# Reordering the output projection of the mixing stage inside a hand-ordered attention loop

## The chip, the cores and the metric

One core of one Trainium2 chip runs the whole program. The metric is the device time of one execution in microseconds. The engines are named as in the profile: PE is TensorE (matrix multiplications), DVE is VectorE, ACT is ScalarE, POOL is GpSimd, and SP issues the loads of the weights.

## The reference

Two transformer blocks run one after the other on 512 tokens of width 1024. The change lies in the first block, in its mixing stage. There the normed and modulated tokens `hx` go through `w_mix_in`; 512 of the columns become queries (8 heads of 64), 256 become two heads of keys and values, and 1536 feed a gated short convolution. The attention result `a` (512 wide) and the convolution's result `sc` (512 wide) are normed separately, laid side by side and multiplied by `w_mix_out` (1024 by 1024):

```python
a = latent_attention(apply_rope(q, cos, sin), apply_rope(k, cos, sin), v, kc, vc)
sc = gb * short_conv3(gc * u, conv_w[l])
mix = jnp.concatenate([rmsnorm(a, attn_out_norm[l]), rmsnorm(sc, conv_out_norm[l])], axis=-1)
x = x + m[:, :, 5] * (mix @ w_mix_out[l])
```

So the product falls into two halves that may be added to `x` in either order: the attention's half uses rows 0 to 511 of `w_mix_out`, the convolution's half rows 512 to 1023. What follows is a gated feed-forward layer (`w_ffn2_in`, `w_ffn2_out`) on the normed `x`.

## The kernel before

All of it is one function, `build`, that issues instructions in an order written out by hand; each engine runs its own in that order. `x` is held transposed as `xT` (8 blocks of 128 features by 512 tokens). Tokens 0 to 255 are the slice `XA`, tokens 256 to 511 the slice `XB`. A product in full precision is made of three half-precision ones, so a block of 128 outputs of one half of `w_mix_out` (`mm3`, four pairs of operands) takes 12 matmuls: of 512 columns for all tokens, of 256 columns for one slice.

**Weights.** `wload` puts a unit of 1 MB into a queue. A load starts when one of two staging buffers is free. `pump_one` issues one step of a unit's split into high and low parts: two on ACT (high), two on DVE (low), and after the last one the staging buffer goes to the next load. A split needs one of four (later six) free result buffers, and `done` frees one. `pump_split` issues a whole split. The order of the queue around the change: nine units of `w_mix_in`, the units `("mixo", 1, n)` (convolution's half of `w_mix_out`), then `("mixo", 0, n)` (attention's half), then the feed-forward's `("f2", ch, g)`.

**The attention loop.** It has 35 iterations, i = 0 to 34, for 4 tiles of 128 tokens by 8 heads. Iteration i issues the scores of pair i (PE, then the row maximum on DVE, line 1092), the exponential of pair i-1 (ACT), the transposition of pair i-2 (six on PE into banks 4 and 5, each bank of three copied out as a high part by ACT and a low part by DVE), and the product with the values of pair i-3 (18 matmuls of 64 columns on PE). Between the transpositions and the product with the values it calls `step(gm)` twice, and at its end `pump_one` once, except in the iterations listed in `NOP`. In the iterations listed in `SK` no `step(gm)` is done.

**The generator `gemms`** is what `step(gm)` advances, by one `yield` each. It computes the convolution's branch (48 yields), the sum of squares over features (a product with `ones`, then `Sqrt`, then two reciprocals of 256 tokens on DVE), the scaling and split of the branch's four blocks (`k`), and the convolution's half of `w_mix_out` in eight blocks (`n`): `mm3` in one yield, and in the next the DVE operation `stt(xT[:, n], ...)` that scales the product and adds it to `xT`. Within the loop every product of `gemms` goes to one PSUM bank, number 7 (`gbk.items[:] = [banks[7]]`). Counting the yields: 16 are used ahead of the loop, and two in each iteration outside `SK`. The product with `ones` falls in iteration 19, the `Sqrt` in 20, the reciprocals in 20 and 21, the scalings in 22 to 25, the convolution's half in 26 to 33, with `mm3` in the first step of each iteration and its scaling in the second. `at_T(0)` and `at_T(1)`, the transpositions of the attention's first two tiles, lie in iterations 22 and 23. They use banks 4 and 5 in turn with the loop's transpositions.

**Behind the loop** come `squares` and `norm_at` for tiles 2 and 3, then `proj(n, XA)` for n = 0 to 7 over eight banks, each a block of the attention's half for the first 256 tokens (12 matmuls of 256 columns, the scaling on DVE, and the square on ACT that POOL adds to the sum of squares), with `at_T(2)` and `at_T(3)` between them. Then `pump_lo` finishes an open split, and `proj(n, XB)` runs for n = 0 to 7, with `rstd(XA)` behind n = 0 and the norm of the next stage's `XA` between the others (`modnorm_x`), and one `pump_split` at n = 7. Then `ffn("f2")` begins.

Of the kernel before, what the change touches and what calls it, by code (L numbers as in the profile page):

```python
# [20 lines left out]
T = 512  # L21
# [38 lines left out]
Z = (8, 2, 2, 2, 2)  # L60
PL = (0, 1, 0, 1)
SK = (4, 10, 15)
NOP = (17, 18, 19, 20, 21)
TWO = ()
FX, NP1, NP2 = 3, 2, 1
WP1, WP3 = 2, 1
NDT = 4
# [150 lines left out]
def build(tc, A, cst, coff, uoff, out, stop=None, dbg=None):  # L218
# [8 lines left out]
    V, S, G, PE, SP = nc.vector, nc.scalar, nc.gpsimd, nc.tensor, nc.sync  # L227
# [5 lines left out]
    def al(n, top=False):  # L233
        n = max(8, -(-n // 8) * 8)
        for i in (range(len(holes) - 1, -1, -1) if top else range(len(holes))):
            o, m = holes[i]
            if m >= n:
                if top:
                    holes[i] = (o, m - n)
                    b = Buf(arena[:, o + m - n:o + m], o + m - n, n)  # L240
                else:
                    holes[i] = (o + n, m - n)
                    b = Buf(arena[:, o:o + n], o, n)
                if holes[i][1] == 0:
                    holes.pop(i)
                return b
        raise MemoryError(f"arena: {n} wanted, {holes}")

    def fr(*bs):
        for b in bs:  # L250
            holes.append((b.off, b.n))
        holes.sort()
        i = 0
        while i + 1 < len(holes):
            if holes[i][0] + holes[i][1] == holes[i + 1][0]:
                holes[i] = (holes[i][0], holes[i][1] + holes[i + 1][1])
                holes.pop(i + 1)
            else:
                i += 1
# [5 lines left out]
    banks = [psum[:, i] for i in range(8)]  # L265
# [38 lines left out]
    def stt(o, a, s, b, op0, op1):  # L304
        V.scalar_tensor_tensor(o, a, s, b, op0=op0, op1=op1)  # L305
# [112 lines left out]
    def wload(key, scale=WS):  # L418
        n, src = unit(key)
        info[key] = (n, scale)  # L420
        q_load.append((key, lambda b: SP.dma_start(b.f(n), src)))
# [14 lines left out]
    rst = al(768).f(768)  # L436
# [15 lines left out]
    xT, cT = b_x.f(KT, T), b_c.f(KT, TC)  # L452
# [28 lines left out]
    XA, XB, XC = slice(0, 256), slice(256, 512), slice(512, 768)  # L481

    def ssq(r_, src, first, e=None):
        if first:
            act(r_, src, AF.Square)
        else:
            t = tmp()[:, :src.shape[-1]]
            act(t, src, AF.Square)
            tt(r_, r_, t, ADD, e)
# [38 lines left out]
    def step(g, n=1):  # L528
        for _ in range(n):
            if next(g, 1):  # L530
                return

    def drain(g):
        for _ in g:
            pass
# [198 lines left out]
    b_raw, b_hl, b_got, pp = [], [], [], [0, 0]  # L734
# [100 lines left out]
        wload(("mix", ch))  # L835
    for t in range(2):
        for n in range(2):
            wload(("mixo", 1 - t, n))
    for ch in range(11):
        for g in range(2):  # L840
            wload(("f2", ch, g))
# [54 lines left out]
    GE_ = [G if x else V for x in PL]  # L896
    tbk, rbk, gbk = Rot(banks[0:4]), Rot(banks[4:6]), Rot([banks[2], banks[3], banks[0], banks[1]])
# [84 lines left out]
    for a in range(2):  # L982
        b = tbk()
# [7 lines left out]
    for a in range(NT):  # L991
        b, b2 = tbk(), tbk()
# [19 lines left out]
    b_gc, b_cu, b_sc = al(2 * 512), al(4 * 514), al(2048)  # L1012
    cu, scn = b_cu.f(4, 514), b_sc.f(4, T)
# [4 lines left out]
    def gemms():  # L1018
        for kind, ch in (("c", 5), ("u", 7), ("c", 6), ("u", 8), ("b", 3), ("b", 4)):
            w = need(("mix", ch))  # L1020
            for q in range(2):
                b, w_, x_ = gbk(), wk(w, KT, 256, P * q), hk(hx)
                mm3(b, w_[0:4], x_[0:4], True, False)
                yield
                yield
                mm3(b, w_[4:8], x_[4:8], False, True)
                yield
                n = 2 * ((ch - 3) % 2) + q
                if kind == "c":
                    act(b_gc.f(2, 512)[:, q], b, scale=IW)  # L1030
                elif kind == "u":
                    stt(cu[:, n, 1:513], b, IW, b_gc.f(2, 512)[:, q], MUL, MUL)
                    act(scn[:, n], cu[:, n, 1:513], scale=col("conv_w", 4 + n))
                    stt(scn[:, n], cu[:, n, 0:512], col("conv_w", n), scn[:, n], MUL, ADD)
                    stt(scn[:, n], cu[:, n, 2:514], col("conv_w", 8 + n), scn[:, n], MUL, ADD)
                else:
                    stt(scn[:, n], b, IW, scn[:, n], MUL, MUL)
                    ssq(rst[:, 0:512], scn[:, n], n == 0, GE_[0])
                if q:
                    done(("mix", ch))  # L1040
                yield
        yield
        b, r_ = gbk(), rst[:, 0:512]
        mm(b, ones, r_)
        squares([0, 1])
        yield
        yield
        act(r_, b, AF.Sqrt, bias=eps, scale=1.0 / 512)
        norm_at(0, 2)
        V.reciprocal(rst[:, XA], rst[:, XA])  # L1050
        yield
        yield
        V.reciprocal(rst[:, XB], rst[:, XB])
        yield
        for k in range(4):
            t = tmp()
            stt(t, scn[:, k, :], col("conv_out", k), r_, MUL, MUL)
            split(t, h2[0][:, 4 + k], h2[1][:, 4 + k], GE_[3])
            yield
            if k < 2:  # L1060
                at_T(k)
            yield
        for n in range(KT):
            b, w = gbk(), wk(need(("mixo", 1, n // 4)), 4, 512, P * (n % 4))
            mm3(b, w, hk(h2)[4:8])
            yield
            stt(xT[:, n], b, mcv[:, 2, n:n + 1], xT[:, n], MUL, ADD)
            if n % 4 == 3:
                done(("mixo", 1, n // 4))
            yield  # L1070
# [64 lines left out]
    def at_T(a):  # L1135
        at, b = b_at[a].f(512), pbk()
        for k in range(4):
            tr(b[:, P * k:P * k + P], at[:, P * k:P * k + P])
        split(b.rearrange("p (k t) -> p k t", k=4), h2[0][:, 0:4, P * a:P * a + P], h2[1][:, 0:4, P * a:P * a + P])


    def proj(n, cs, b):
        w = wk(need(("mixo", 0, n // 4)), 4, 512, P * (n % 4))
        o = b[:, 0:256]
        mm3(o, w, hk(h2, cs)[0:4])
        stt(xT[:, n, cs], o, mcv[:, 2, n:n + 1], xT[:, n, cs], MUL, ADD)
        ssq(rst[:, cs], xT[:, n, cs], n == 0, G)

    gm, qh = gemms(), q_heads(0)
    step(gm, Z[0])  # L1150
# [12 lines left out]
    for i in range(8 * NT + 3):  # L1163
        if i < 8 * NT:
            sc_.append(scores(i // 8, i % 8))
        if sc_ and i:
            ex.append(expo(*sc_.pop(0)))
        if ex and i > 1:
            pt_.append(ptrans(*ex.pop(0)))
        fill = i not in SK  # L1170
        step(gm, fill)
        if i < 24 and i % 8 == 0:
            qh = q_heads(1 + i // 8)
        step(gm, fill)
        if pt_ and i > 2:
            pv(*pt_.pop(0))
        step(qh)
        for _ in range(0 if i in NOP else 2 if i in TWO else 1):
            pump_one()
    drain(gm)  # L1180
    squares([2, 3])
    norm_at(2, 2)
    mbk = Rot([banks[i] for i in (7, 0, 1, 2, 3, 6, 7, 0)])
    for n in range(8):
        proj(n, XA, mbk())
        if n == 2:
            at_T(2)
        if n == 5:
            at_T(3)
    checkpoint("sc", b_sc.f(2048))  # L1190
    checkpoint("mx", h2[0])
    fr(b_ro, b_t1, b_t2, *b_q2, b_k2, b_k, b_sm, b_rp, b_gc, b_cu)
# [3 lines left out]
    na, mbk = None, Rot([banks[i] for i in (1, 2, 3, 0, 5, 6, 7, 2)])  # L1196
# [55 lines left out]
    b_lg = al(8 * 12, top=True)  # L1252
# [10 lines left out]
    b_kc, b_cn, b_T, b_gu, b_r2, b_M, b_Q = al(8), al(512), al(768), al(512), al(512), al(512), al(1024)  # L1263
# [172 lines left out]
    for a, _ in enumerate(tokproj("rv", hx, range(NT), to_act(rv))):  # L1436
# [4 lines left out]
        else:  # L1441
            d = a - 2
            b = sb_()
# [54 lines left out]
    b_la, b_lac, b_gk, b_gqT, b_gkc, b_L = (al(n) for n in (2048, 1024, 1024, 1024, 512, 6 * P))  # L1498
# [9 lines left out]
    b = sb_()  # L1508
# [8 lines left out]
    for i in range(2):  # L1517
        b = tb()
        n = 4 - 2 * i
# [5 lines left out]
    for i in range(6):  # L1525
        b = lbk()
# [24 lines left out]
    b_A, b_qd = [al(512) for _ in range(2)], [al(512) for _ in range(2)]  # L1551
# [45 lines left out]
    b_e = [al(512) for _ in range(2)]  # L1597
    for a, _ in enumerate(tokproj("gk", hx, range(NT), to_act(gk))):
        step(rc)
        if a < 2:  # L1600
            o = la[:, 2 * a:2 * a + 2]
            tt(o, o, t6[a + 1], SUB)
        if a == 1:
            fr(*b_t6[1:])
            b_yr = al(2048)
            yr = (b_yr.h(4, T), b_yr.h(4, T, at=4 * T))
    units_done("gk")
    w = need(("in", 8))
    for p in range(2):
        b = pb()  # L1610
# [10 lines left out]
    b_gvc, b_gv, b_gkT = al(1024), al(2048), al(1024)  # L1621
    gvc, gv, gkT = b_gvc.f(2, 512), b_gv.f(NT, 512), b_gkT.f(2, T)
    bSG = {(0, 0): al(512), (1, 3): al(512)}
# [83 lines left out]
    b_gg = al(2048)  # L1707
# [82 lines left out]
    for n in range(KT):  # L1790
        w = wk(need(("wout", n // 2)), KT, 256, P * (n % 2))
        b = pb()
# [4 lines left out]
            pump_one()  # L1797
    drain(gc_)
    checkpoint("yg", yg[0])
    fr(*b_A, *b_km, *b_qm, *b_e, b_yr, b_gv, b_gg, b_la, b_gqT, b_gkT, *b_X, *bSG.values(), b_T, b_gu, b_lg)  # L1800

    ring(spl_free, len(spl_free) + 2)
    coef(0, "norm2", m23, 4, 0)
# [149 lines left out]
    gbk = Rot(banks[4:8])  # L1953
# [432 lines left out]
        tail_T(KT - 1, a)  # L2386
    tail_out([1, 2, 3])
    es.close()
    print('pp', pp)

# [23 lines left out]
```

## Time and profile before

| | |
|---|---|
| median of 3 runs | 2669.93 us (2669.27 to 2672.03) |
| profiled execution | 2673.24 us, span 2671.5 us |
| PE busy | 2597.3 us (97%) |
| DVE busy | 2017.4 us (76%) |
| ACT busy | 1070.0 us (40%) |
| POOL busy | 534.0 us (20%) |
| mean granted PE clock | 0.994 |

The busy shares are means over the span. In the slices of the page PE is at nine tenths nearly everywhere; the attention loop lies at about 648 to 789 us, and what the change touches lies between 715 and 860 us. Times in the rows count from the span's start. A bracket at the end of a timeline's line gives how long the engine idled ahead of it and what released it.

### The profile page before, as it was taken

The numbers are of one execution on the slowest core, as the hardware profiler recorded it, in microseconds if no ns is written. First come the engines' busy times: TensorE is split into PE (matmuls) and PEld (weight loads), VectorE is DVE, ScalarE is ACT, GpSimd is POOL, SyncE is SP. The second block draws the span as 40 slices with busy tenths as digits, with TensorE's granted clock in tenths as the row PEclk, the third lists the DMA queues.
The fourth block names the chain that finished last, engine by engine and source line by source line (L and its number), as shares of the span: only waits on it lengthen the run. The fifth ranks groups of instructions, "written<-read, shape, count | busy, mean of one in ns | idle before, by whom it ended". The sixth has DMA issues, their size and how long they took to land. (4 is left out here: it accounts for less than half of the span.)

```text
span 2671.5 us, 43737 instructions
## 1 busy us (share of the span) xinstructions
PE 2597.3 (97%) x17395; PEld 1650.2 (62%) x17395; DVE 2017.4 (76%) x3604; ACT 1070.0 (40%) x1671; POOL 534.0 (20%) x637
## 2 busy tenths in 40 slices
PE   7999999999989999999999999999999999999998
PEld 3666666675566444479787655576566666666665
DVE  6888547876877786676535787998799777787885
ACT  3544322145655443543434675344333222222224
POOL 1000000001011000011002476123223333333330
PEclk9999999999999999999999999999999999999999
DMA  6698628522105788744211598778999999999982
GB/s 271 225 340 333 216 107 302 188 75 99 49 33 213 278 310 289 271 164 137 74 64 48 194 374 291 275 283 290 375 372 370 395 353 353 349 357 364 357 305 82
DMA packets 209585, 656.09 MB, mean 246 GB/s; under 512 B 19010, under 2 KB 85348, under 8 KB 188900
## 3 DMA queue, kind: packets, MB, share of 16 engines
q1 hardware_dynamic: 156388, 452.68, 46.0%
q0 software_dynamic: 44352, 188.76, 20.1%
q10 hardware_dynamic: 8640, 11.85, 1.2%
q8 instruction: 136, 2.23, 0.3%
q14 instruction: 69, 0.57, 0.1%
HBM read 549.81 MB, written 103.42 MB: 245 GB/s over the span
## 5 line engine op out<-in xcount | busy, mean ns | idle before, releaser
L279 PE MATMUL psum<-arena 128*128 128x384 f16 (+8 forms) x16840 | 2549.3, 313 | 43.1 <-ACT arena L293 21.7
L279 PEld LDWEIGHTS <-arena 128*128 128x128 f16 x16116 | 1500.8, 98 | 925.3 <-issue 24.5
L293 ACT ACTIVATE arena<-arena 128x1024 f16<-128x1024 f32 (+11 forms) x1026 | 743.4, 765 | 1170.0 <-DVE arena L305 922.1
L305 DVE SCALAR_TENSOR_TENSOR arena<-arena 128x1024 f16<-128x1024 f32 (+7 forms) x1240 | 1065.4, 895 | 137.9 <-ACT arena L293 114.6
L308 DVE TENSOR_TENSOR arena<-arena 128x1024 f16<-128x1024 f16 (+11 forms) x668 | 377.6, 589 | 116.1 <-ACT arena L293 98.3
L293 ACT ACTIVATE arena<-psum 128x512 f32<-128x512 f32 (+8 forms) x522 | 263.4, 528 | 403.2 <-PE psum L279 328.4
L308 POOL TENSOR_TENSOR arena<-arena 128x8 f32<-128x8 f32 (+4 forms) x284 | 191.8, 702 | 743.3 <-ACT arena L293 283.3
L305 DVE SCALAR_TENSOR_TENSOR arena<-psum,arena 128x384 f32<-128x384 f32 (+4 forms) x293 | 171.7, 589 | 216.0 <-PE psum L279 178.5
L2166 POOL DMA_INDIRECT arena<-in_peer_down_dram,arena x128 | 130.7, 1021 | 291.2 <-DVE arena L2172 263.4
L2166 POOL DMA_INDIRECT arena<-in_peer_up_dram,arena x128 | 126.6, 989 | 228.8 <-DVE arena L305 216.0
L2172 DVE SCALAR_TENSOR_TENSOR arena<-arena 128x1024 f32<-128x1024 f32 x128 | 155.9, 1219 | 2.1 <-DMA arena<-in_peer_down_dram,arena 2.0
L425 POOL DMA_DIRECT2D arena<-in_units_dram x52 | 27.9, 536 | 645.9 <-DVE arena L305 640.6
L279 PEld LDWEIGHTS psum<-arena 128*128 128x128 f32 (+1 forms) x724 | 94.1, 185 | 48.5 <-issue 19.4
L282 PE MATMUL psum<-arena 128*128 128x128 f32 (+2 forms) x555 | 76.7, 269 | 23.1 <-DVE arena L308 14.6
L282 PEld LDWEIGHTS psum<-arena 128*128 128x128 f32 (+1 forms) x493 | 57.2, 141 | 29.7 <-DVE arena L308 13.3
L1915 DVE MAX8 arena<-arena 128x8 f32<-128x128 f32 (+1 forms) x192 | 42.9, 260 | 36.1 <-POOL arena L308 31.2
L2104 POOL COPY arena<-arena 128x128 f32<-128x128 f32 x24 | 45.9, 1940 | 114.3 <-ACT arena L293 114.3
L308 DVE TENSOR_TENSOR arena<-psum,arena 128x384 f16<-128x384 f32 (+3 forms) x95 | 52.3, 579 | 17.5 <-ACT arena L293 9.2
L1918 DVE FIND_INDEX8 arena<-arena 128x8 uint32<-128x128 f32 (+1 forms) x192 | 47.9, 264 | 0.0
L293 ACT ACT_TABLE_LOAD x33 | 42.3, 1283 | 11.1 <-PE psum L279 8.5
L293 ACT ACTIVATE arena<-psum,arena 128x768 f32<-128x768 f32 (+4 forms) x54 | 39.6, 735 | 12.6 <-PE psum L279 6.6
L1092 DVE TENSOR_REDUCE arena<-psum 128x1 f32<-128x768 f32 x32 | 30.4, 950 | 6.8 <-PE psum L279 6.8
(54 smaller groups left out, 212.8 us busy)
## 6 DMA issues: line engine op xcount, KB each, us to landing
arena<-in_units_dram SPq DMA_DIRECT2D x91, 1024.0 KB
arena<-dscr SPq DMA_DIRECT2D x128, 512.0 KB
arena<-in_units_dram SPq DMA_DIRECT2D x128, 512.0 KB
arena<-in_down_t_dram SPq DMA_DIRECT2D x120, 512.0 KB
dscr<-arena SPq DMA_DIRECT2D x120, 512.0 KB
arena<-in_units_dram POOLq DMA_DIRECT2D x52, 1024.0 KB
gscr<-arena SPq DMA_DIRECT2D x12, 1920.0 KB
arena<-gscr SPq DMA_DIRECT2D x30, 768.0 KB
```

Source lines behind the costliest of these rows:

```text
L279: PE.matmul(o, l, r, start=start, stop=stop)
L282: PE.transpose(o, i, (ident if i.dtype == F32 else ident16)[:i.shape[0], :i.shape[0]])
L293: S.activation(o, i, f, **kw)
L305: V.scalar_tensor_tensor(o, a, s, b, op0=op0, op1=op1)
L308: (e or V).tensor_tensor(o, a, b, op=op)
L425: q_raw.append((key, lambda b: eng.dma_start(b.f(n), src)))
L1092: V.tensor_reduce(n[:, 0:1], s_, axis=mybir.AxisListType.XY, op=ALU.max, negate=True)
L1915: V.max(v[:, c_], x)
L1918: V.max_index(i[:, c_], v[:, c_], x)
L2104: G.tensor_copy(b_Gt[hf].f(NB, 4, 32)[:, nb], Gs[:, 4 * hf:4 * hf + 4])
L2166: G.indirect_dma_start(out=held[job].f(D), out_offset=None, in_=W["peer_up_2" if job[0] else "peer_down_2"], in_offset=bass.IndirectOffset ...
L2172: V.scalar_tensor_tensor(row, row, 1.0, acc, op0=MUL, op1=MUL, accum_out=c_[:, j:j + 1])
```

## The change

The attention's half for `XA` moves from behind the loop into the generator, between the four scalings of the convolution's branch; `proj` writes it into the two halves of bank 7 in turn. The convolution's half comes after it, and its blocks n = 5 to 7 behind the loop, over banks 0, 1, 2, 3, 7. The squares for the sum over `XA` are now taken from the convolution's blocks. The sum of squares of the convolution's branch goes to `b_gc`. The two `mixo` pairs change places in the load queue. `NOP` loses 17 and 18, and from iteration 33 on no step of the generator is made. In a later stage a buffer of 2048 is asked for as two of 1024.

```diff
-NOP = (17, 18, 19, 20, 21)
+NOP = (19, 20, 21)
+END = 33
...
-            wload(("mixo", 1 - t, n))
+            wload(("mixo", t, n))
...
-                    ssq(rst[:, 0:512], scn[:, n], n == 0, GE_[0])
+                    ssq(b_gc.f(512), scn[:, n], n == 0, GE_[0])
...
-        b, r_ = gbk(), rst[:, 0:512]
+        b, r_ = gbk(), b_gc.f(512)
         mm(b, ones, r_)
         squares([0, 1])
         yield
         yield
         act(r_, b, AF.Sqrt, bias=eps, scale=1.0 / 512)
         norm_at(0, 2)
-        V.reciprocal(rst[:, XA], rst[:, XA])
         yield
+        at_T(0)
         yield
-        V.reciprocal(rst[:, XB], rst[:, XB])
+        V.reciprocal(r_[:, XA], r_[:, XA])
+        at_T(1)
         yield
+        V.reciprocal(r_[:, XB], r_[:, XB])
+        yield
+
         for k in range(4):
+            proj(2 * k, XA, half(), False)
+            yield
             t = tmp()
             stt(t, scn[:, k, :], col("conv_out", k), r_, MUL, MUL)
             split(t, h2[0][:, 4 + k], h2[1][:, 4 + k], GE_[3])
             yield
-            if k < 2:
-                at_T(k)
+            proj(2 * k + 1, XA, half(), False)
             yield
         for n in range(KT):
             b, w = gbk(), wk(need(("mixo", 1, n // 4)), 4, 512, P * (n % 4))
             mm3(b, w, hk(h2)[4:8])
             yield
             stt(xT[:, n], b, mcv[:, 2, n:n + 1], xT[:, n], MUL, ADD)
+            ssq(rst[:, XA], xT[:, n, XA], n == 0, G)
             if n % 4 == 3:
                 done(("mixo", 1, n // 4))
             yield
...
-    def proj(n, cs, b):
+    half = Rot([banks[7][:, 0:256], banks[7][:, 256:512]])
+
+    def proj(n, cs, b, last=True):
...
-        ssq(rst[:, cs], xT[:, n, cs], n == 0, G)
+        if last:
+            ssq(rst[:, cs], xT[:, n, cs], n == 0, G)
...
-        fill = i not in SK
+        fill = i not in SK and i < END
...
-    drain(gm)
     squares([2, 3])
     norm_at(2, 2)
-    mbk = Rot([banks[i] for i in (7, 0, 1, 2, 3, 6, 7, 0)])
-    for n in range(8):
-        proj(n, XA, mbk())
-        if n == 2:
-            at_T(2)
-        if n == 5:
-            at_T(3)
+    gbk.items[:] = [banks[i] for i in (0, 1, 2, 3, 7)]
+    step(gm, 6)
+    at_T(2)
+    drain(gm)
+    at_T(3)
...
-            b_yr = al(2048)
-            yr = (b_yr.h(4, T), b_yr.h(4, T, at=4 * T))
+            b_yr = [al(1024) for _ in range(2)]
+            yr = tuple(b.h(4, T) for b in b_yr)
```

## Rows read from the trace of the kernel before

**Rows 1.** The page: span, and busy time of each engine.
```profile
span 2671.5 us, 43737 instructions
PE 2597.3 (97%) x17395; PEld 1650.2 (62%) x17395; DVE 2017.4 (76%) x3604; ACT 1070.0 (40%) x1671; POOL 534.0 (20%) x637
```

**Rows 2.** Windows: stretch, length, PE, PEld, DVE, ACT, POOL busy, PE clock, DMA.
```profile
731.00:744.00 13.00, 7.65 (x74) 5.54 (x74) 10.06 (x14) 9.76 (x17) 1.16 (x1) 0.87 0.00 0
744.00:757.00 13.00, 9.53 (x103) 6.42 (x102) 10.91 (x16) 8.89 (x19) 3.20 (x3) 1.00 0.00 1
757.00:777.00 20.00, 19.90 (x188) 12.38 (x187) 13.51 (x22) 10.93 (x24) 0.76 (x1) 1.00 0.14 53
```

**Rows 3.** Timeline of iterations 21 to 25 (start, length, engine, line).
```profile
737.68 1.74 DVE L1053 RECIPROCAL arena<-arena 128x256 f32<-128x256 f32 x1
...
745.82 0.66 PE L282 MATMUL psum<-arena 128*128 128x128 f32 x4 [1.14 <-DVE arena L308]
...
753.93 1.02 DVE L308 TENSOR_TENSOR arena<-psum,arena 128x384 f16<-128x384 f32 x2
754.87 1.88 DVE L305 SCALAR_TENSOR_TENSOR arena<-arena 128x512 f32<-128x512 f32 x2
756.66 0.95 DVE L1092 TENSOR_REDUCE arena<-psum 128x1 f32<-128x768 f32 x1
```

**Rows 4.** Timeline of iteration 30, with a block of the convolution's half.
```profile
771.70 0.75 DVE L305 SCALAR_TENSOR_TENSOR arena<-psum,arena 128x512 f32<-128x512 f32 x1 [1.36 <-PE psum L279]
...
772.68 0.82 PE L282 MATMUL psum<-arena 128*128 128x128 f32 x6
772.88 0.96 DVE L1092 TENSOR_REDUCE arena<-psum 128x1 f32<-128x768 f32 x1 [0.42 <-PE psum L279]
773.21 0.87 ACT L293 ACTIVATE arena<-psum 128x384 f16<-128x384 f32 x2 [1.08 <-PE psum L282]
...
773.33 3.93 PE L279 MATMUL psum<-arena 128*128 128x512 f16 x34
773.75 1.01 DVE L308 TENSOR_TENSOR arena<-psum,arena 128x384 f16<-128x384 f32 x2
...
776.12 0.75 DVE L305 SCALAR_TENSOR_TENSOR arena<-psum,arena 128x512 f32<-128x512 f32 x1 [1.36 <-PE psum L279]
...
777.30 0.96 DVE L1092 TENSOR_REDUCE arena<-psum 128x1 f32<-128x768 f32 x1 [0.42 <-PE psum L279]
```

**Rows 5.** Timeline behind the loop.
```profile
785.36 7.73 PE L279 MATMUL psum<-arena 128*128 128x512 f16 x84
...
789.20 0.69 DVE L308 TENSOR_TENSOR arena<-psum,arena 128x512 f32<-128x512 f32 x1 [0.19 <-PE psum L279]
...
792.55 1.41 DVE L305 SCALAR_TENSOR_TENSOR arena<-arena 128x512 f32<-128x512 f32 x2
...
793.85 4.09 PE L279 MATMUL psum<-arena 128*128 128x256 f16 x36
...
800.10 0.48 DVE L305 SCALAR_TENSOR_TENSOR arena<-psum,arena 128x256 f32<-128x256 f32 x1
...
803.68 9.87 PE L279 MATMUL psum<-arena 128*128 128x256 f32 x86 [1.37 <-POOL arena L308]
...
806.02 1.75 DVE L495 RECIPROCAL arena<-arena 128x256 f32<-128x256 f32 x1 [0.85 <-ACT arena L293]
```

**Rows 6.** Timeline of the feed-forward's second pair of units.
```profile
838.46 46.78 PE L279 MATMUL psum<-arena 128*128 128x512 f16 x216 [1.04 <-ACT arena L293]
...
840.78 5.77 DVE L305 SCALAR_TENSOR_TENSOR arena<-arena 128x1024 f16<-128x1024 f32 x5 [0.26 <-ACT arena L293]
843.16 0.33 SPq L421 DMA_DIRECT2D arena<-in_units_dram  x1
...
848.99 2.95 ACT L293 ACTIVATE arena<-arena 128x1024 f16<-128x1024 f32 x3 [1.18 <-DMA arena<-in_units_dram]
```

**Rows 7.** Windows of PE alone: stretch, length, busy, PE clock, DMA.
```profile
739.00:744.00 5.00, 3.25 (x28) 0.66 0.00 0
```

More of the change, by code (lines that the diff above doesn't have):

```diff
@@ L1799, in build @@
     checkpoint("yg", yg[0])
-    fr(*b_A, *b_km, *b_qm, *b_e, b_yr, b_gv, b_gg, b_la, b_gqT, b_gkT, *b_X, *bSG.values(), b_T, b_gu, b_lg)
+    fr(*b_A, *b_km, *b_qm, *b_e, *b_yr, b_gv, b_gg, b_la, b_gqT, b_gkT, *b_X, *bSG.values(), b_T, b_gu, b_lg)
     ring(spl_free, len(spl_free) + 2)
@@ L2388, in build @@
     es.close()
-    print('pp', pp)
 _INS = ["q_norm", "k_norm", "attn_out_norm", "ret_decay_f_2", "ret_decay_b_2", "gla_gk_up_f_2", "gla_gk_bias_f_2",
```

## The prediction

> **What bounds the kernel now.** I read the page first: TensorE is busy 97% of the span and no other engine comes near it [rows 1], so a reordering can gain only where TensorE idles or where a chain hangs on one engine. The windows of the attention loop come next [rows 2]: from 731 to 757 us TensorE works 17.2 of 26 us, from 757 to 777 us 19.9 of 20. The first stretch holds the root and the scalings of the convolution's branch, the second the convolution's half of w_mix_out. The reader is to see holes of 8.8 us in the first stretch and none in the second. The timeline gives the reasons. In the holes VectorE sets the pace: from the maximum at 753.02 (one pattern ahead of that at 756.66) an iteration is maximum 0.9, two low parts 0.95, a scaling with a weight's low part 1.8, with no gap, 3.6 us [rows 3]; the reciprocals of 1.74 us and the waits of TensorE for a bank (1.14 us at 745.82) fall there too [rows 3]. In the second stretch an iteration takes 4.42 us from maximum to maximum (772.88 to 777.30), and TensorE has no gap although every block uses one bank: a block's scaling is issued in the same iteration (771.70), long before the next block's multiplication (773.4) [rows 4].
>
> **The change part by part.** Sums are differences inside the profiled execution (2673.24 us, span 2671.5), added to the median of 2669.93, 3.3 us below it.
>
> *Prices.* A block for the first 256 tokens is 12 of the 36 matmuls that took 4.09 us, 1.3 us; a block of the convolution's half twice that, 2.6 us; scalings 0.45 and 0.75 us of VectorE [rows 4, 5]. Eight blocks (10.4 us) go from behind the loop into it; three of the convolution's (7.8 us) go the other way.
>
> *Iterations 20 to 28.* Iteration 20 loses a reciprocal, so the maximum of 21 comes at 734.3 instead of 1.7 us later. Iteration 21 now has both transpositions of tiles 0 and 1 with a reciprocal between their splits. After the maximum VectorE waits to 736.4 for the exponential's table, as it does now, then low parts 1.0, a wait of 0.85 for transposition and copy, split 0.65, reciprocal 1.74 [rows 3], split 0.65: the maximum of 22 at 741.3. From there I add VectorE's own work: 22 has maximum 0.9, low parts 1.0, reciprocal 1.74, projection 0.45, 4.1 in all; 23 and 24 each 0.9, 1.0, 0.7, 0.45 and a weight's low part 1.2, 4.25; 25 has two projections, 2.75; 26 a scaling, a projection and the 0.9 us that closes tile 2, 3.85; 27 3.0. The maximum of 28 comes at 763.5, now at 764.04 (777.30 less three periods [rows 4]). So seven blocks, 9 us of TensorE, disappear in the holes: that is what the change can earn.
>
> *Iterations 28 to 32.* Here the order turns. Counting yields, 62 stand ahead of the convolution's half now and 67 after the change: an odd number. Multiplication and scaling change places: the first step of an iteration scales block n-1, the second multiplies block n, both on bank 7. The multiplication must wait for a scaling that stands on VectorE behind this iteration's maximum and two low parts, which wait for this iteration's transpositions. By iteration 30 [rows 4]: transpositions end at 773.4, low parts at 774.76, the scaling would end at 775.45, the multiplication start at 775.5 in place of 773.4. TensorE idles 2.1 us, and behind it queue the values' product and the next scores, on which the next maximum waits. From multiplication to next maximum it is 3.9 us now, so a period becomes 6.6 to 6.7 instead of 4.42. In 28 the block waits for the last projection's scaling, itself behind the exponential that the last split held up: 767.05 against a free TensorE at 764.35. The maxima: 29 at 771.05 (768.46 now), 30 at 777.75 (772.88), 31 at 784.35 (777.30). From there: wait and block 3 to 5.2, values 0.65, transpositions 0.65, wait 2.1, block 4 2.6, values 0.65, then transpositions, values, a wait of 0.75 for the last low part and the last values: 14.5 us, so the loop ends at 798.9 where it now ends at 789.1 (the closing of tile 3 at 789.20 [rows 5]): **+9.8**.
>
> *The two halves of a bank.* In 25 two projections follow each other in different halves. No row shows a matmul writing one half while VectorE reads the other. If this is free, nothing is added; if the second waits for the first's scaling (755.8 to 756.2 behind the low parts), carrying this through to 29 gives 2.0 us. No row is nearer to either end, so I take the middle, **+1.0**. The Trainium skill, "PSUM — Partial Sum Buffer", section "PSUM bank collisions raise a hardware error", says to guard by bank and quadrant and not by address: by it this term would be 2.0 and the sum 2687. No row shows it.
>
> *Behind the loop.* Now: reciprocal of the first tokens' root at 806.02, 16.9 us after the loop's end [rows 5]. After: block 4's scaling stands behind the norm of tiles 2 and 3, which ends 4.9 us after the loop (the two at 792.55 end at 793.96) [rows 5], so at 5.65. The bank for block 6 is again number 7 (the 20th call takes item 19 modulo 5 of banks 0, 1, 2, 3, 7), so TensorE waits from 2.6 to 5.7. Block 6 to 8.3, block 7 to 10.9, both transpositions to 12.1, split of tile 2 to 12.9, block 7's scaling 13.65, its square 14.1, split of tile 3 15.4, the first block for the last tokens 16.7; the open low part, its scaling, square and root bring the reciprocal to 18.5: **+1.6**. If VectorE holds the split back less, or the wait for bank 7 is covered, it can be 1.5 us below now; the upper end is 3.
>
> *Weights.* Four result buffers stay in use, but the convolution's first unit is freed in iteration 32 instead of 29 and the second behind the loop. So one feed-forward unit fewer is split when that layer starts: two, where there are three now. The second pair starts at 838.46; now its first unit is ready, and the splitting that begins at 840.78 makes its second, whose end at 843.16 starts the next load [rows 6]. After the change that split makes the first: its first half is done at 842.0, so TensorE waits **+3.6**. The load behind it lands in time, as now at 848.99 [rows 6]. Lower end 0, where TensorE's start is already later for its bank; upper end 5. The earlier pump in 18 only moves a split from 25 to 18. The swapped order of the load queue issues the same loads at the same completions, so no queue waits longer. The split buffer of the later stage and the sums on POOL (busy 20% [rows 1]) I cost at nothing; were POOL late, the root behind the loop would wait as it does now (1.37 us at 803.68 [rows 5]).
>
> Sum: 9.8 + 1.0 + 1.6 + 3.6 = 16.0, so **2686 us**. What follows is bound by TensorE for most of its length (97% over the span [rows 1]), so I expect nothing to give it back.
>
> **The rivals.** *Faster:* the wait of the odd order is covered, VectorE reaching the scaling before TensorE needs it, so that blocks 0 to 4 run at 4.42 us an iteration. The loop then ends 0.5 us earlier than now; without the bank wait of block 6 the tail gains 1.5 to 2.6; the low clock of 739 to 744 (0.66 of full over 5 us [rows 7], 1.7 us of work) goes with the fuller holes. That gives 4 to 6 us, 2664. For it speak the holes; against it that low parts and scaling stand on one queue [rows 4]. It decides below a wait of some 0.3 us per block. Chance 0.10. *No change:* the wait is only about 0.5 us, five times 0.5 and 1.6 less the 0.5: some 4 us, 2673.5, the units in time. Chance 0.13. *Clock:* the idle of 2.1 in 6.6 us lowers the clock for the block behind each gap; at half rate a block costs 2.6 more, twice or three times 2.6 us: 2692. Against it: TensorE kept its full clock from 744 to 757 at 9.5 of 13 us busy [rows 2], though it fell just before after idling more [rows 2, 7]. The Trainium skill, "TensorE: Matmul & The Clock Gate", section "A second HAM failure mode: psum-queue depth-cycling", names idling between groups of multiplications as a cause of such swings; by it this case would hold, and the stretch from 744 to 757 does not agree. Chance 0.07.
>
> **How the numbers follow.** The forecast has 0.70. Its own range: the loop 7 to 12, the bank 0 to 2, the tail -1.5 to 3, the weights 0 to 5; not all ends at once, so 2678 to 2691. With part of the no-change case and the clock's, 2673.5 to 2692 holds 8 in 10. A measurement can tell about 0.2%, 5.3 us: faster 0.10, same 0.13, slower 0.77.
>
> **What would show it.** Right: gaps of about 2 us on TensorE, released by VectorE's scaling, in front of blocks 1 to 4; periods near 6.6 us from maximum 29 on; the maximum of 28 hardly moved; a wait of some 3 us for bank 7 behind the loop; a wait of some 3.6 us at the feed-forward's second pair. Wrong: periods of 4.4 us in 29 to 31 with no such gap, or a maximum of 28 more than 3 us off.

## The result and the profile after

The changed kernel takes 2703.99 us (median of 4 runs, 2700.51 to 2704.73) against 2669.88 us before: ratio 1.0122, 95% interval 1.011 to 1.0134. The forecast had the sign and most of the mechanisms, but 16 of 34 us, and the result lies above its range. The span of the profiled execution grows from 2671.5 to 2702.9 us, by 31.4; the account below is made inside the two spans.

The windows of the changed kernel, in the columns of [rows 2], for the same stretches and one more:

```profile
731.00:744.00 13.00, 8.44 (x61) 6.63 (x61) 8.74 (x14) 9.57 (x17) 0.00 (x0) 0.74 0.00 0
744.00:757.00 13.00, 10.55 (x131) 9.14 (x130) 12.61 (x19) 7.99 (x17) 3.21 (x2) 1.00 0.11 33
757.00:777.00 20.00, 16.77 (x171) 12.96 (x169) 11.29 (x21) 7.17 (x16) 2.32 (x2) 0.91 0.08 33
777.00:789.00 12.00, 9.32 (x68) 4.80 (x68) 3.19 (x5) 3.47 (x8) 0.73 (x1) 0.86 0.00 0
```

From 731 to 757 TensorE is now busy 19.0 us where it was busy 17.2. Only part of that is filled holes: from 731 to 744 it runs fewer matmuls than before (61 against 74) and at a lower clock (0.74 against 0.87), from 744 to 757 more of them (131 against 103) at the full clock. But from 757 to 777, where it had no gap, it idles 3.2 us and runs 9% below its full clock; from 777 to 789 VectorE and ScalarE work about 3 us each of 12 and TensorE still idles. So the idle time there is a chain, not a load.

Iteration 25, the timeline of VectorE and TensorE (it has the projections of blocks 3 and 4):

```profile
755.19 1.02 DVE L309 TENSOR_TENSOR arena<-psum,arena 128x384 f16<-128x384 f32 x2
...
756.13 0.48 DVE L306 SCALAR_TENSOR_TENSOR arena<-psum,arena 128x256 f32<-128x256 f32 x1
...
756.66 4.28 PE L280 MATMUL psum<-arena 128*128 128x256 f16 x34 [2.45 <-DVE arena L306]
759.07 0.48 DVE L306 SCALAR_TENSOR_TENSOR arena<-psum,arena 128x256 f32<-128x256 f32 x1 [2.46 <-PE psum L280]
...
760.98 0.96 DVE L1099 TENSOR_REDUCE arena<-psum 128x1 f32<-128x768 f32 x1 [1.43 <-PE psum L280]
761.43 2.65 PE L280 MATMUL psum<-arena 128*128 128x256 f16 x34
```

Block 4's multiplication writes the other half of bank 7, and still starts at 756.66, 0.05 us after the scaling of block 3 ends (756.13 and 0.48). The group then takes 4.28 us; the same 34 matmuls take 2.65 us in the next iteration (761.43). They ran at the lower clock: the granted clock was 0.79 from 754 to 762, in the windows further down.

Iterations 29 and 30, the same view (compare [rows 4]):

```profile
777.65 3.93 PE L280 MATMUL psum<-arena 128*128 128x512 f16 x34 [1.98 <-DVE arena L306]
...
781.62 0.96 DVE L1099 TENSOR_REDUCE arena<-psum 128x1 f32<-128x768 f32 x1 [4.01 <-PE psum L280]
782.00 0.87 ACT L294 ACTIVATE arena<-psum 128x384 f16<-128x384 f32 x2 [3.07 <-PE psum L283]
782.53 1.02 DVE L309 TENSOR_TENSOR arena<-psum,arena 128x384 f16<-128x384 f32 x2
783.47 0.74 DVE L306 SCALAR_TENSOR_TENSOR arena<-psum,arena 128x512 f32<-128x512 f32 x1
784.26 5.61 PE L280 MATMUL psum<-arena 128*128 128x512 f16 x34 [2.03 <-DVE arena L306]
```

Read downward: maximum, high parts, low parts, scaling of the last block, and only then the next multiplication, 2.03 us after TensorE was free. VectorE meanwhile waits 4.0 us for TensorE. Each waits for the other once an iteration. The block behind the third such wait in a row (after those ahead of 771.09 and 777.65) takes 5.61 instead of 3.93 us.

Behind the loop and at the feed-forward's start, the same view:

```profile
804.29 0.69 DVE L309 TENSOR_TENSOR arena<-psum,arena 128x512 f32<-128x512 f32 x1 [0.36 <-PE psum L280]
...
809.77 5.34 PE L280 MATMUL psum<-arena 128*128 128x512 f16 x24 [2.92 <-DVE arena L306]
...
823.21 1.75 DVE L496 RECIPROCAL arena<-arena 128x256 f32<-128x256 f32 x1 [0.85 <-ACT arena L294]
...
837.41 2.92 DVE L306 SCALAR_TENSOR_TENSOR arena<-arena 128x1024 f16<-128x1024 f32 x2 [1.49 <-ACT arena L294]
837.43 0.61 PE L280 MATMUL psum<-arena 128*128 128x256 f16 x2 [4.97 <-ACT arena L294]
...
839.26 22.54 PE L280 MATMUL psum<-arena 128*128 128x256 f16 x189 [1.22 <-DVE arena L306]
...
865.17 0.60 PE L280 MATMUL psum<-arena 128*128 128x512 f16 x2 [3.38 <-ACT arena L294]
866.43 33.93 PE L280 MATMUL psum<-arena 128*128 128x512 f16 x149 [0.65 <-DVE arena L306]
```

Before the change the feed-forward's first product stood at 814.78; the same view of TensorE:

```profile
814.78 5.42 PE L279 MATMUL psum<-arena 128*128 128x256 f16 x48 [1.24 <-DVE arena L305]
```

The last loop output stands 15.1 us later than before (804.29 against 789.20 [rows 5]), the reciprocal 17.2 (823.21 against 806.02 [rows 5]). Then TensorE waits 4.97 and 1.22 us for the two halves of a weight's split (837.41): the feed-forward's first product needs two units, and the second is split only at block 7. After two matmuls at 837.43 it runs from 839.26, where before it ran from 814.78: 24.5 us late. The second pair runs from 866.43, 28.0 us late [rows 6], after waits of 3.38 and 0.65 us for the two halves of its first unit.

The windows of TensorE alone, in the columns of [rows 7], round five places where its clock was low:

```profile
754.00:762.00 8.00, 5.55 (x48) 0.79 0.36 133
784.00:790.00 6.00, 5.74 (x37) 0.72 0.00 0
818.00:824.00 6.00, 5.04 (x31) 0.72 0.40 135
834.00:844.00 10.00, 5.35 (x32) 0.66 0.44 165
865.00:871.00 6.00, 5.18 (x16) 0.72 0.42 113
```

Length times the share missing is about 1.7 us in four of them (8 times 0.21, 6 times 0.28) and 3.4 us in the one from 834 to 844, where TensorE idles nearly half of the time anyway. Each stands behind a wait of TensorE: four behind waits shown above, the one at 818 behind a wait of 2.62 us for ScalarE's split of tile 3.

### The profile page after: what moved, and what is told of

Same layout as the page of the kernel before. It is cut to its first block, busy times and chain, and to the rows that moved or that the text cites. A ratio compares the mean times of both kernels' runs of the same rounds, so it can differ in the third digit from the quotient of the medians.

```text
span 2702.9 us, 43736 instructions
## 1 busy us (share of the span) xinstructions
PE 2607.5 (96%) x17395; PEld 1655.3 (61%) x17395; DVE 2016.3 (75%) x3604; ACT 1069.3 (40%) x1671; POOL 531.3 (20%) x637
## 5 line engine op out<-in xcount | busy, mean ns | idle before, releaser
L280 PE MATMUL psum<-arena 128*128 128x384 f16 (+7 forms) x16840 | 2559.1, 314 | 66.3 <-ACT arena L294 30.2
```

The lines of the kernel that those rows point to most:

```text
L280: PE.matmul(o, l, r, start=start, stop=stop)
```

## The experiments

**One empty step in the kernel before.** Nothing else is changed, so the fuller iterations and the weights' order play no part.

```diff
+        yield
         for n in range(KT):
             b, w = gbk(), wk(need(("mixo", 1, n // 4)), 4, 512, P * (n % 4))
```

> The kernel before with one empty yield ahead of the convolution's half, so that a block's multiplication moves to the second step of an iteration and its scaling to the first step of the next; nothing else. Theory (the odd count is a cost of its own): TensorE waits about 2.0 us for VectorE's scaling ahead of blocks 1 to 7, 14 us, and 0 to 6 us more where the clock falls behind a wait: 2684 to 2691 us. Rival (the waits come from the moved projections or from the fuller iterations, not from the order): within 2 us of 2670.

It took 2687.82 us, ratio 1.007 (1.0053 to 1.0087), and 2690.81 us, 1.007 (1.0047 to 1.0093), in a second set of runs:

> The kernel before with the one empty yield again, beside the run with the filling matmuls on the same chip: 2684 to 2691 us, with two blocks at the low clock.

The timeline of TensorE in the first set:

```profile
775.58 3.92 PE L279 MATMUL psum<-arena 128*128 128x512 f16 x34 [1.98 <-DVE arena L305]
782.14 5.61 PE L279 MATMUL psum<-arena 128*128 128x512 f16 x34 [1.98 <-DVE arena L305]
...
802.24 9.42 PE L279 MATMUL psum<-arena 128*128 128x512 f16 x84 [1.97 <-DVE arena L305]
```

Seven waits of 1.98 us and two groups 1.7 us longer than their likes (5.61 against 3.92, 9.42 against 7.73 [rows 5]). 13.9 and 3.4 make 17.3 of the 18.1 us of the first set. The order of two steps alone does this.

**The same with the waits filled.** Ten matmuls whose results nobody reads, into banks that the next scores overwrite, ahead of each block but the first:

```diff
             b, w = gbk(), wk(need(("mixo", 1, n // 4)), 4, 512, P * (n % 4))
+            for _ in range(10 if n else 0):
+                mm(psum[:, 2 * ((at_i[0] + 1) % 2), 0:384], qT[:, 0, 0:P], kT[:, 0, 0, 0:384])
             mm3(b, w, hk(h2)[4:8])
...
+    at_i = [0]
...
+        at_i[0] = i
```

> The kernel before with the one empty yield, and ahead of blocks 1 to 7 ten more matmuls of 384 columns, 1.6 us, into the banks that the next scores overwrite; their results are not used. They lie inside the wait of 2.0 us. Theory (the clock falls because TensorE idles, and that is 1.7 us each time): all periods from maximum to maximum are 6.6 us, none 8.3, the granted clock stays 1.00 from 760 to 810, 3 us less than the run without these matmuls, 2683 to 2686 us. Rival (the slow block has another cause, or the matmuls only push the waits on): a period of over 8 us remains, 2687 us or more.

2684.22 us (2683.08 to 2685.19), 1.0053 (1.0035 to 1.0071): 3.6 and 6.6 us less than the two sets without them. The times leave it loose, because the intervals overlap and one of the eight executions without the filling took 2683.13 us. The traces, one of each set, say more. The timeline of TensorE:

```profile
775.21 3.92 PE L279 MATMUL psum<-arena 128*128 128x512 f16 x34 [0.36 <-DVE arena L305]
781.77 3.93 PE L279 MATMUL psum<-arena 128*128 128x512 f16 x34 [0.36 <-DVE arena L305]
...
800.19 7.73 PE L279 MATMUL psum<-arena 128*128 128x512 f16 x84 [0.34 <-DVE arena L305]
```

The idle time shrinks to 0.36 us, the starts still stand 6.56 us apart, and both slow groups are gone. The feed-forward's second pair starts at 853.27, in the two sets without the filling at 857.03 and 857.42. One window of TensorE alone, first from this run, then from the second set without the filling:

```profile
783.00:796.00 13.00, 12.30 (x101) 1.00 0.00 0
```

```profile
783.00:796.00 13.00, 9.77 (x76) 0.88 0.01 1
```

So in these traces the low clock is a consequence of the idling, and it is a cost of its own on top of the wait.

**The order restored in the changed kernel.**

```diff
+        yield
         for n in range(KT):
...
-    step(gm, 6)
+    step(gm, 7)
```

> The changed kernel with one empty yield ahead of the convolution's half, which restores multiplication first, scaling second; one block more stands behind the loop. Theory: the waits of 2.0 us ahead of blocks 0 to 4 go, and with them the low clock of block 2 (1.7 us) and the 2.9 us wait for bank 7 behind the loop: 11 to 14 us less, 2690 to 2693 us. Rival (the loss lies in the projections' iterations and the weights): 2701 to 2704 us.

2688.80 us, 1.007 (1.0053 to 1.0086): 15.2 us less than the change, 1.2 more than the expected 11 to 14. All waits ahead of the convolution's blocks are gone, and so is the one for bank 7 behind the loop; the one of iteration 25 and that for the weights stay. The timeline of TensorE:

```profile
756.68 4.28 PE L280 MATMUL psum<-arena 128*128 128x256 f16 x34 [2.45 <-DVE arena L306]
...
775.54 3.93 PE L280 MATMUL psum<-arena 128*128 128x512 f16 x34
...
823.32 0.61 PE L280 MATMUL psum<-arena 128*128 128x256 f16 x2 [4.96 <-ACT arena L294]
825.14 22.80 PE L280 MATMUL psum<-arena 128*128 128x256 f16 x189 [1.22 <-DVE arena L306]
```

**An earlier split in the changed kernel.**

```diff
-PB = (7,)
+PB = (1, 7)
```

> The changed kernel with one more split of a weight unit, at block 1 of the last tokens' projection, where a result buffer is free. Theory (the feed-forward starts 7.3 us late because its second unit is split only at block 7, and its second pair 3.5 us late): both waits go, the split costs about 2.5 us of VectorE in the norm's chain, 7 to 10 us less: 2694 to 2697 us. Rival (the start hangs on the norm's chain, the unit is late without being waited for): 2704 to 2707 us.

2693.08 us, 1.0084 (1.0068 to 1.0101): 10.9 us less, 0.9 more than the expected 7 to 10. The feed-forward starts at 835.81, after a wait of 3.72 us for VectorE (1.24 before), so the split costs 2.5 us in the norm's chain; the second pair starts without a wait for weights. The timeline of TensorE:

```profile
835.81 23.23 PE L280 MATMUL psum<-arena 128*128 128x256 f16 x194 [3.72 <-DVE arena L306]
860.08 20.23 PE L280 MATMUL psum<-arena 128*128 128x512 f16 x93 [1.04 <-ACT arena L294]
```

**Both together,** with `gbk.items` cut to banks 0 to 3 behind the loop.

> The changed kernel with the empty yield ahead of the convolution's half and the earlier split of a weight unit, and bank 7 left out behind the loop. Theory (order and weights are separate costs that add): 15.2 and 10.9 us less than 2704, 2677 to 2680 us, the rest being the two projections of iteration 25 and the split in the norm's chain. Rival (both cure the same lateness at the feed-forward's start): 2686 to 2689 us.

2678.53 us, 1.0033 (1.002 to 1.0046). 15.2 and 10.9 off 2704.0 make 2677.9: within the intervals they add, and are two causes.

**The later stage's buffer,** as two in the kernel before.

> The kernel before with the later stage's buffer of 2048 as two of 1024; nothing else. Theory (it costs nothing): 2669 to 2671 us. Rival (of the 3.4 us that the changed kernel loses after the feed-forward's second pair, a part comes from other addresses): 2672 to 2673.5 us.

2670.74 us, ratio 1.000 (0.999 to 1.001): no cost.

**One projection an iteration.** From the run with both cures: the scaling of a block k ahead of projection k+1, the last three projections with an empty step each, `END = 35`, bank 7 again among the banks behind the loop, and there

```diff
-    step(gm, 7)
-    at_T(2)
-    drain(gm)
-    at_T(3)
+    step(gm, 4)
+    at_T(2)
+    at_T(3)
+    drain(gm)
```

> The same, with at most one projection in an iteration (22 to 29) and the steps of the loop up to its end, so that blocks 0 to 4 of the convolution's half lie in iterations 30 to 34; the transpositions of tiles 2 and 3 go ahead of block 7. Theory (two projections in one iteration cost 2.4 us and a low clock of 1.7 us because both write one bank): 4 to 8 us less than the run without this, 2669 to 2675 us. Rival (the halves of the bank are free of each other, the wait was VectorE's own work): no more than 2 us less.

2672.49 us, 1.001 (1.0001 to 1.0019): 6.0 us less. In the trace the step from maximum 25 to 26 falls from 5.05 us (754.76 to 759.81) to 2.85 us (754.39 to 757.24), so the wait for the bank was worth 2.2 us; the low clock that I had added to it was not there in the run with both cures (its group after the wait took 2.65 us). The other 3.8 us are not traced to one place: this run rearranged the later iterations and the part behind the loop as well, and the second pair starts 4.5 us earlier (844.89 in the run with both cures). So the total does not test the halves; the step does. What is left is a wait of 4.72 us for VectorE ahead of the first product (1.24 before). The second unit's early split now stands in the norm's chain there, 2.36 us of VectorE after 1.13 us of waiting for ScalarE's part; the timeline of VectorE and TensorE:

```profile
810.86 2.36 DVE L306 SCALAR_TENSOR_TENSOR arena<-arena 128x1024 f16<-128x1024 f32 x2 [1.13 <-ACT arena L294]
...
816.11 23.23 PE L280 MATMUL psum<-arena 128*128 128x256 f16 x194 [4.72 <-DVE arena L306]
840.39 39.87 PE L280 MATMUL psum<-arena 128*128 128x512 f16 x184 [1.04 <-ACT arena L294]
```

**Only four projections moved, the rest as before.** As in the change, the branch's sum of squares goes to `b_gc`; the squares of blocks 0 to 3 are taken from the convolution's blocks.

```diff
         norm_at(0, 2)
-        V.reciprocal(rst[:, XA], rst[:, XA])
         yield
+        at_T(0)
         yield
-        V.reciprocal(rst[:, XB], rst[:, XB])
+        V.reciprocal(r_[:, XA], r_[:, XA])
+        at_T(1)
+        V.reciprocal(r_[:, XB], r_[:, XB])
         yield
...
-            if k < 2:
-                at_T(k)
+            proj(k, XA, banks[7], False)
...
-    for n in range(8):
+    for n in range(4, 8):
```

> The kernel before with only four of the eight projections of the first tokens moved, one into each of the scalings' iterations 22 to 25, the transpositions of tiles 0 and 1 into iteration 21; the convolution's half stays where it was, the weights' queue too, and blocks 4 to 7 stay behind the loop. Theory (the holes are worth what TensorE can fill without a new wait): the loop ends 0 to 1 us later, the part behind it is up to 5 us shorter, 2664 to 2668 us. Rival (the tail hangs on the norm of tiles 2 and 3 and its chain, not on TensorE): 2669 to 2672 us.

2672.29 us, 1.0008 (0.9999 to 1.0017): 0.3 us above the rival's range, 4.3 above the theory's. Neither holds whole. Maximum 28 stands at 767.61, 3.6 us later than before, since two reciprocals and the splits of two tiles in one iteration push maximum 22 from 739.34 to 743.15; that cost comes from the rearranged iteration 21 and not from the filled holes. The part behind the loop is 3.6 us shorter and no more: TensorE has less to do, then waits 2.48 us for ScalarE's split of tile 3 and goes on at the low clock. The second pair starts where it started before (838.50 against 838.46). The timeline of TensorE, and under it a window of TensorE alone:

```profile
801.81 0.27 PE L279 MATMUL psum<-arena 128*128 128x256 f16 x1 [2.48 <-ACT arena L293]
...
838.50 41.82 PE L279 MATMUL psum<-arena 128*128 128x512 f16 x193 [1.04 <-ACT arena L293]
```

```profile
804.00:806.00 2.00, 2.00 (x10) 0.50 0.35 53
```

**All cures.** The spread version with `PB = (7,)` again, the result buffers enlarged right behind the loop, and the second unit's split put where VectorE waits:

```diff
+    fr(b_ro, b_t1, b_t2, *b_q2, b_k2, b_k, b_sm, b_rp, b_gc, b_cu)
+    ring(spl_free, 6 - len(ready))
     squares([2, 3])
+    pump_lo()
     norm_at(2, 2)
+    pump_hi()
...
     step(gm, 4)
+    pump_one()
     at_T(2)
...
-    fr(b_ro, b_t1, b_t2, *b_q2, b_k2, b_k, b_sm, b_rp, b_gc, b_cu)
```

> The run with the projections spread, with the result buffers enlarged and the second weight unit of the feed-forward split right behind the loop, its VectorE part where VectorE waits for the root's table and for the blocks; no early split among the last tokens' blocks. Theory (of that run's parts only the 4.7 us wait for the second unit, with its low clock, was left against the before): 4 to 7 us less than it, 2665 to 2669 us, 0.1 to 0.2% faster than before. Rival (VectorE's parts push the norm's chain back by as much): 2671 to 2674 us.

2668.43 us, ratio 0.9994 (0.9985 to 1.0003). The second pair starts at 836.12, 2.3 us earlier than before, and the median is 1.5 us lower; that is no measurable gain. It keeps the change's load order and its `NOP`, so these two cost nothing that it shows. It removes the whole loss of the change, and shows how little there was to win:

```profile
818.66 16.42 PE L280 MATMUL psum<-arena 128*128 128x256 f32 x146 [0.81 <-POOL arena L309]
836.12 44.19 PE L280 MATMUL psum<-arena 128*128 128x512 f16 x204 [1.04 <-ACT arena L294]
```

## Why the prediction was wrong in size

Two steps of the prediction failed. *Weights* counted the feed-forward's second unit as ready when the layer starts: it was not, and the first product came 7.3 us later for it. *Clock* argued that idling like this leaves the clock alone: it fell, which cost 3.4 us in the loop. Beside them the term of the bank was too small by 1.0 us, and 3.4 us behind the second pair were put at nothing. The sign that the prediction named for being wrong came: maximum 28 stands at 767.59, 3.6 us later than the 764.04 before and 4.1 later than the 763.5 forecast.

| Step of the prediction | Forecast, us later than before | Trace |
|---|---|---|
| end of the loop, with the bank's middle | 10.8 | 15.1 |
| behind the loop, to the reciprocal | 1.6 | 2.1 |
| first product of the feed-forward | 0 | 7.3 |
| its second pair | 3.6 | 3.5 |
| from there to the end | 0 | 3.4 |
| sum | 16.0 | 31.4 |

The point on the clock rests on one more row, from the timeline of TensorE before the change:

```profile
740.75 1.11 PE L282 MATMUL psum<-arena 128*128 128x128 f32 x4 [2.38 <-DVE arena L308]
```

- **The odd order was right,** in place, price and reason: waits of 1.98 to 2.03 us (forecast 2.1), shown alone in the kernel before, and gone when the order is restored.
- **The bank's two halves.** I took the middle of 0 and 2.0 us for want of a row. The matmul waited for the scaling of the other half, so the upper end held, 1.0 more; the later run without two projections in one iteration gives 2.2 for it. The Trainium skill, "PSUM — Partial Sum Buffer", section "PSUM bank collisions raise a hardware error", gives a guard by bank; the 2.45 us wait agrees with it. The wait is one that the program makes, and no run lets the two halves be used at the same time.
- **The clock is the term that I gave to a rival with 0.07.** In the loop it cost 1.7 us in iteration 25 and 1.7 us in block 2. With the bank's 1.0 that is about the loop's missing 4.3 us. The step that failed was the argument from one stretch, 744 to 757, that idling like this leaves the clock alone. That stretch had TensorE busy 73%, and its longest gap was 1.14 us [rows 3]. The one before, with the low clock of [rows 7], had a gap of 2.38 us and was the nearer row for waits of 2.0 us (740.75 above). The Trainium skill, "TensorE: Matmul & The Clock Gate", section "A second HAM failure mode: psum-queue depth-cycling", names such swings behind idling; the run with filled waits agrees. The rival had the event, a low clock behind two waits of the loop, but priced it at 2.6 us each where 1.7 came.
- **The weights: the mechanism was right, its first place was missed.** I counted two units ready when the layer starts. But the second is split at block 7 of the last tokens, whose split on VectorE begins at 837.41, after the point where the norm allows the first product (reciprocal 823.21 plus the 8.8 us from 806.02 to 814.78, so 832.0). The first product needs both units. That is 7.3 us, the largest part of what the forecast missed; the run with the earlier split shows it. The second pair's wait came as forecast.
- **Behind the loop** the wait for bank 7 was 2.92 us (forecast 3.1).
- **The last 3.4 us.** One low stretch at 865 to 871 accounts for 1.7. The rest stays open: behind the second pair the runs' spans move by -5.0 (the filled waits) to +3.4 us (the change) against the before, with no part of it that I could tie to one place. The buffer of the later stage is not it.
- **The gain was small.** With the order kept, four moved projections shortened the part behind the loop by 3.6 us, and the loop lost as much in iteration 21. What the filled holes are worth without that loss no run shows alone; with all cures the second pair starts 2.3 us earlier.
- **A sum of the faster rival is off:** 0.5, 1.5 to 2.6 and 1.7 us make 3.7 to 4.8, not 4 to 6. Nothing hangs on it.

## What to carry to other kernels

When work is put into a hand-ordered software pipeline, count the steps ahead of what follows: an odd number turns "multiply, then empty the bank" into "empty, then multiply", and a single bank that cost nothing becomes a wait every round. Follow the buffers that a moved step frees to the first consumer that needs all of them, not to the next one in the list. And price an idle TensorE at more than its length: behind some of the waits here part of the following block also ran at the lower clock.

## What the runs showed of the hardware

The clock of TensorE did not fall behind every wait of 2.0 us. With the one empty step there are seven equal waits of 1.98 us, the blocks behind them starting 5.9 to 8.3 us apart; in the profiled execution of both sets the clock fell behind the fourth and the seventh, each time for 1.7 us of lost work. With 1.6 us of matmuls put into each wait, leaving 0.36 us idle, it stayed at 1.00 in every window from 757 to 810 (from 783 to 796 TensorE was busy 12.30 us of 13, against 9.77 at 0.88). The length of one wait does not decide it either: behind the wait of 2.45 us in iteration 25 the same 34 matmuls took 4.28 us in the changed kernel and 2.65 us in the run with both cures.
